# A trunk layer's second feed-forward half-step: one fp32 copy on another engine, and two pieces of work behind a later anchor

## The chip, the cores and the metric

The kernel runs on one core of a Trainium2 chip. A core has a matrix engine (TensorE, PE in the profile, with its weight loads shown as PEld), VectorE (DVE), ScalarE (ACT), GpSimd (POOL) and SyncE (SP), which here only issues DMAs. Each engine works through its own list of instructions in order and waits on semaphores for the others. The metric is the device time of one execution in microseconds (us); of several runs the median counts.

## The reference

One layer of a diffusion trunk on 512 latent and 128 context tokens, model width 1024: a half-step SwiGLU feed-forward, a token mixer (differential attention beside a chunkwise mLSTM), and a second half-step SwiGLU. Each stage is modulated by shifts, scales and gates that come from a conditioning vector. The change lies at the entry of the second half-step, which is

```python
hh = rmsnorm(x, g[2]) * (1 + m[7]) + m[6]
x = x + 0.5 * m[8] * swiglu(hh, p['ffn2_w1'][l], p['ffn2_w3'][l], p['ffn2_w2'][l])
...
def swiglu(h, w1, w3, w2):
    return (jax.nn.silu(h @ w1) * (h @ w3)) @ w2
```

with an inner width of 2816. All arrays are fp32.

## The kernel before

**Layout.** Activations lie transposed: feature d of the model in 8 tiles of 128 partitions, the 640 tokens along the free dimension, cut in two halves of 320 (`HALF`). The second half holds 192 latent and 128 context tokens, which have different shifts and scales; so `SEGS` (line 27) cuts every modulated operation of the second half in two, 192 and 128 long. The residual lies in four pair tiles (`x_pairs`, line 1764), each two feature tiles.

**Three matmuls for one.** TensorE works on rounded values (`F32R`). Each operand is split into a high part (a rounded copy, ScalarE) and a low part (value minus high part, VectorE), and `mm3` (line 133) or `into` (line 393) multiplies high by high, high by low and low by high. A value's low part needs the value itself in fp32 and its high part.

**The feed-forward.** The inner width is cut into 11 blocks of 256. Block 0 is done plainly: four sums (two column groups f, two weight matrices i) for each token half, each over 8 feature tiles k with three matmuls each (`plain`, line 313). The later blocks 1 to 10 use a Strassen-Winograd scheme with seven products in place of eight (`products`, line 406): A11, S1, S2, A12, S3, A22, S4. The operands on the activation side are four quarters (2 halves of the features by 2 halves of the tokens) and four sums of them, S1 to S4 (`operand_sums`, line 330); these sums are made in place in the fp32 residual pairs, so an fp32 copy of the modulated activations must stand there first. `terms` makes one sum on VectorE and its high part on ScalarE; `low` makes its low part on VectorE. S4 is kept in the tiles of the quarter (0, 1), the first features of the second token half, which block 0's plain products read.

On the weight side a **granule** is one 256 column block of w1 or w3 (`Granule`, line 232): `load` fetches 1 MB into one of two `raw` buffers, `parts` makes the split weights `wB` and `wC` and edits `raw` into the weight sums, and `sums` splits those into `ww`. `split_at` is the VectorE instruction that ends `sums` (line 268). Granule i+1's `parts` and `sums` are issued in the midst of granule i's products. In the stream of TensorE the last two products of a granule, A22 and then S4, come inside the next granule: A11, S1, A22 of the one before, S2, S4 of the one before, A12, S3. A product is 12 matmuls. Copies u2 and u3 of a PSUM bank (`copy_of`, line 401) are taken by ScalarE between products that go on accumulating in the same bank (Y); the sum for S1 with u3 is read by VectorE out of bank Z before S4 is added there.

Outputs of a block are gated (`SO`, SiLU of one times the other), split into `g` (`store_g`, line 372) and stored to `g_dram`, from which the second matrix's part, the "down" products, reads them much later. The residual was stored to `x2_dram` before it was overwritten, and is read back into `x_pairs` (line 1870) for the same later part.

**Entry of the second half-step.** `out_units(hf)` (line 1812) makes the mixer's output projection for one token half, adds it to the residual and collects the squares for the norm. `normed(hf)` (line 1825) turns them into the reciprocal root `rs`, multiplies the pairs by it in place (line 1834, VectorE), and then for each feature tile and segment has ScalarE write, with shift and scale, the rounded copy into `hm` (line 1838) and the fp32 copy in place (line 1839); VectorE subtracts the two for the low part of a pair (line 1841). `normed(1)` is issued after the first k of block 0's plain products for the first token half; the products for the second half follow.

**What sets the order.** TensorE's instructions keep the program's order (`keep_in_program_order`). For the other engines a scheduler orders the instructions by its own estimate of the times; `issue_after(x)` holds instructions of x's engine behind x. In `operand_sums` every VectorE instruction but the last two, the lows of S4, is chained to the one before it; the low of S2's second half is handed on as `behind`, which holds the second granule's `parts`.

Of the kernel before, what the change touches and what calls it, by code (L numbers as in the profile page):

```python
# [10 lines left out]
AF = mybir.ActivationFunctionType  # L11
ALU = mybir.AluOpType
# [19 lines left out]
def tile_trunk(ctx: ExitStack, tc: tile.TileContext, a: dict):  # L32
    nc = tc.nc
    act = nc.scalar.activation
# [9 lines left out]
    def ts(out, in0, s1, op0, s2=None, op1=None):  # L44
        if s2 is None:
            vec.tensor_scalar(out=out, in0=in0, scalar1=s1, scalar2=None, op0=op0)
        else:
            vec.tensor_scalar(out=out, in0=in0, scalar1=s1, scalar2=s2, op0=op0, op1=op1)
# [55 lines left out]
    scale = cp.tile([128, 3, KT, 2], F32, name="scale")  # L104
# [118 lines left out]
    A11, S1, S2, A12, S3, A22, S4, A21 = range(8)  # L223
# [71 lines left out]
    class HalfStep:  # L295
# [31 lines left out]
            act(s, p[0], AF.Silu)  # L327
            tt(vec, self.SO[:, self.Q[f, hf]], p[1], s, ALU.mult)

        def operand_sums(self, pair):  # L330

            SS = {i: self.fp.tile([128, 2, 4, HALF], F32R, tag=f"s{i}", name="S") for i in (S1, S2, S3)}
            SS[S4] = self.part[0, 1]
            self.ops = {A11: self.part[0, 0], A12: self.part[1, 0], A22: self.part[1, 1], **SS}
            a = [[[pair(2 * kh + r)[:, :, half(hf)] for hf in range(2)] for kh in range(2)] for r in range(2)]

            places = {
                S1: ((1, 1), (0, 1), (1, 1), ALU.add), S3: ((0, 1), (0, 0), (0, 1), ALU.subtract),
                S2: ((0, 0), (1, 1), (0, 0), ALU.subtract), S4: ((1, 0), (1, 0), (0, 0), ALU.subtract),
            }  # L340
            prev = None

            def next_of_vec(*args):
                nonlocal prev
                with ExitStack() as st:
                    if prev is not None:
                        st.enter_context(tc.issue_after(prev.ins))
                    prev = tt(vec, *args)

            def terms(i, r):  # L350
                to, x_, y_, op = places[i]
                v, x_, y_ = (a[r][kh][hf] for kh, hf in (to, x_, y_))
                next_of_vec(v, x_, y_, op)
                act(SS[i][:, 0, 2 * r : 2 * r + 2], v, AF.Copy)

            def low(i, r):
                kh, hf = places[i][0]
                ks = slice(2 * r, 2 * r + 2)
                next_of_vec(SS[i][:, 1, ks], a[r][kh][hf], SS[i][:, 0, ks].bitcast(F32), ALU.subtract)

            for f, i, r in (
                (terms, S1, 0), (terms, S1, 1), (terms, S3, 0), (low, S1, 0), (terms, S2, 0), (low, S1, 1), (terms, S3, 1),
                (terms, S2, 1), (low, S2, 0), (low, S2, 1), (low, S3, 0), (low, S3, 1), (terms, S4, 0), (terms, S4, 1),
            ):
                f(i, r)
                if (f, i) == (low, S2):
                    behind = prev.ins
            low(S4, 0)
            low(S4, 1)
            return behind  # L370

        def store_g(self, SO, b):
# [191 lines left out]
                for f in range(2):  # L564
                    unit(G[-1], j, f, 1)

        def run(self, x, gate, final, behind=None):


            def nothing(*args):  # L570
                pass

            n = self.n_plain
            down = [Whole(n, self.fetch_w2(0, n, j)) for j in range(4)]

            up = self.ops
            at = [[up[i] for i in (A11, S1, S2, A12)], [up[i] for i in (S3, S4, A22)], None]

            def fetch(q, i, eng=nc.sync):
                b0, b1 = ((0, n), *GROUPS)[q]  # L580
                eng.dma_start(out=at[q][i][:, :, : b1 - b0].bitcast(F32), in_=self.g_dram[i, :, :, b0:b1, :])

            work = self.up_work()
            work[-1][3] = lambda i: {A11: lambda: fetch(0, 0), S1: lambda: fetch(0, 1), S2: lambda: fetch(0, 2), A12: lambda: fetch(0, 3)}.get(i, nothing)()
            self.products(work, nothing, down[:2], behind=behind)
            at[1] += [self.fp.tile([128, 2, 4, HALF], F32R, tag=tag, name="op") for tag in ("gA", "SO")] + at[0][:2]
            x = x()

            def down_done(q, j):
                def done(f, hf, p, u):  # L590
                    d = 2 * j + f
                    if u is not None:
                        p = self.add(p, u)
                    add_residual(x, p, d, hf, gate)
                    if q == 2:
                        final(d, hf)

                def used(i):
                    if q == 1 and j == 3 and i in moves:
                        fetch(2, moves[i], nc.gpsimd)  # L600

                return done, used

            last = [
                [Granule(b1 - b0, self.fetch_w2(b0, b1, j)), lambda i, q=q: at[q][i], *down_done(q, j)]
                for q, (b0, b1) in zip((1, 2), GROUPS) for j in range(4)
            ]
            at[2] = at[0][2:] + at[1][:5]

            moves = {A11: S2, S1: A12, S2: S3, A12: A22, S3: S4}  # L610
            for j in range(4):
                ahead = down[j + 2] if j < 2 else last[j - 2][0]
                loaded = ahead.load()
                with tc.issue_after(loaded):
                    for i in ((A11, S1), (S2, A12), (S3,), ())[j]:
                        fetch(1, i)
                if j < 3:
                    down[j + 1].split()
                else:
                    last[0][0].parts(self.fp)  # L620
                    last[0][0].sums()
                for hf in range(2):
                    for f in range(2):
                        p = acc_tile(self.psum)
                        for kh in range(2):
                            op = at[0][PLAIN_Q[kh, hf]]
                            for b in range(n):
                                w = [down[j].w(i, n * kh + b, f) for i in range(2)]
                                mm3(p, *w, op[:, 0, b], op[:, 1, b], kh + b == 0, kh == 1 and b == n - 1)
                        add_residual(x, p, 2 * j + f, hf, gate)  # L630
                    if (j, hf) == (3, 0):
                        for i in (A22, S4):
                            fetch(1, i, nc.gpsimd)

            def load_last(load=last[3][0].load):
                with tc.issue_after(load()):
                    for i in (A11, S1):
                        fetch(2, i)

            last[3][0].load = load_last  # L640
            self.products(last, nothing, prepared=True)
# [51 lines left out]
    with ExitStack() as ph:  # L693
# [9 lines left out]
        hs = HalfStep(1, fp, ntmp, psum, a["w1a"], a["w3a"], a["w2a"], FB)  # L703
# [197 lines left out]
        x = Now()  # L901
# [445 lines left out]
    with tc.issue_after(box["normed"]):  # L1347
# [7 lines left out]
        for i in range(2):  # L1355
            vec.tensor_tensor_reduce(
                out=tab0[:, 3, i, :], in0=lamv[:, 2 * i, :], in1=lamv[:, 2 * i + 1, :], op0=ALU.mult, op1=ALU.add,
                scale=1.0, scalar=0.0, accum_out=ldot[:, i : i + 1],
# [403 lines left out]
    out = ExitStack()  # L1762
    zp = out.enter_context(tc.tile_pool(name="yy", bufs=1))
    x_pairs = pairs("k", "x")
    x = [x_pairs[d // 2][:, d % 2, :] for d in range(KT)]
# [59 lines left out]
    def normed(hf):  # L1825

        if hf == 0:
            natural_log_exp()
        rs = st[hf].rstd(psum)
        c0 = hf * HALF  # L1830
        shift = m_of(6)
        for g in range(4):
            xs = x_pairs[g][:, :, half(hf)]
            tt(vec, xs, xs, rs[:, None, :].to_broadcast([128, 2, HALF]), ALU.mult)
            for d in (2 * g, 2 * g + 1):
                for s0, s1, j in SEGS[hf]:
                    by = dict(scale=scale[:, 2, d, j : j + 1], bias=shift[:, d, j : j + 1])
                    act(hs.hh(d, hf)[0][:, s0 - c0 : s1 - c0], x[d][:, s0:s1], AF.Identity, **by)
                    act(x[d][:, s0:s1], x[d][:, s0:s1], AF.Identity, **by)
            p = hs.part[g // 2, hf][:, :, 2 * (g % 2) : 2 * (g % 2) + 2]  # L1840
            tt(vec, p[:, 1], xs, p[:, 0].bitcast(F32), ALU.subtract)

# [22 lines left out]
                hs.plain(ps[f, i], W[i], f, 1, k)  # L1865
    for f in range(2):
        hs.gate_plain(f, 1, (ps[f, 0], ps[f, 1]))
    summed = hs.operand_sums(lambda r: x_pairs[r])
    for g in range(4):
        nc.sync.dma_start(out=x_pairs[g], in_=x2_dram[:, 2 * g : 2 * g + 2, :])  # L1870
    hs.store_g(hs.SO, 0)
    hs.run(
        lambda: x, half_m[:, 1], lambda d, hf: nc.sync.dma_start(out=a["y"][:, d, half(hf)], in_=x[d][:, half(hf)]),
        behind=summed,
    )


# [126 lines left out]
```

## Time and profile before

| | us |
|---|---|
| median of 3 runs | 1868.25 |
| the three runs | 1867.74, 1868.25, 1875.11 |
| span of the profiled execution, first to last instruction | 1872.4 |
| busy of that: TensorE / VectorE / ScalarE | 1812.7 / 1300.2 / 849.6 |
| block 0's plain products of the second token half, start to first granule | 1459.45 to 1481.20 |

For the profiled execution only the span is given, as its own time. The mean clock granted to TensorE was 0.988 of full speed.

A row of the timeline has start, length, engine, line of the kernel, operation, output and inputs with their shapes, the count of merged instructions, and in brackets how long the engine was idle before it and what ended that. Rows of grouped instructions have after the count the busy time in us, the mean of one in ns, and the idle time before them. Nearly all VectorE operations have the line of a small helper: 39 for two-tensor operations, 42 for scalar_tensor_tensor, 46 and 48 for tensor_scalar; `hm` rows are told apart by their tiles.

### The profile page before, as it was taken

Reading aid. Unit: us, or ns where it says so; the run is one execution under the profiler, and the core shown is the slowest. Engines: PE = TensorE matmul, PEld = TensorE weight load, DVE = VectorE, ACT = ScalarE, POOL = GpSimd, SP = SyncE. Lnnn points to the kernel's source line nnn. Section 1 sums busy time; section 2 is a strip of 40 time slices with the busy share of each in tenths; the row PEclk is TensorE's granted clock in tenths of the full one; section 3 lists DMA queues with packets and bytes.
Section 4 is the critical chain, followed back from the end, with each engine's and each line's share of the span. In section 5 each row is a group of like instructions: output and inputs, shape, how many; then the busy total and the mean of one; then the engine's idle time right before and its main releaser. Section 6 shows DMA issues by size and latency. Waiting matters only on the chain.

```text
span 1872.4 us, 30753 instructions
## 1 busy us (share of the span) xinstructions
PE 1812.7 (97%) x12658; PEld 1774.4 (95%) x12658; DVE 1300.2 (69%) x2177; ACT 849.6 (45%) x1455; POOL 35.8 (2%) x57
## 2 busy tenths in 40 slices
PE   5899999999999999999999989999999999999999
PEld 4899999999998999999999979999999899999999
DVE  6888886576786675865755537875456778887585
ACT  5644444112554353453454436565235645554232
POOL 1000001110000000000000000000000000000000
PEclk8899999999999999999999999999999999999999
DMA  8344547964324322322222254566442344457972
GB/s 328 119 142 168 192 169 260 382 213 146 118 81 133 123 74 95 120 77 95 98 79 83 74 178 128 187 208 218 167 134 95 130 140 153 171 177 250 336 275 91
DMA packets 127293, 299.81 MB, mean 160 GB/s; under 512 B 9457, under 2 KB 90609, under 8 KB 114353
## 3 DMA queue, kind: packets, MB, share of 16 engines
q1 hardware_dynamic: 117890, 257.49, 40.0%
q0 software_dynamic: 9264, 40.37, 5.9%
q8 instruction: 99, 1.62, 0.4%
q14 instruction: 40, 0.33, 0.0%
HBM read 234.20 MB, written 63.63 MB: 159 GB/s over the span
## 4 chain that ended last, share of the span: by engine, by line
PE 86%; DVE 7%; DMA 4%; ACT 2%; issue 1%; SPq 0%; DVEq 0%; ACTq 0%
PE ps_f L52 41%; PE ps_p L52 22%; PE ps_t L52 12%; PE ps_o L52 2%; PE sc L52 2%; PE ps_n L52 2%; PE ps_u L52 1%; DMA ada<-csil_dram 1%; PE ps_wT L55 1%; DVE ww L39 1%; PE ps_qkT L55 1%; DMA P<-nm_dram 1%; DMA so<-o_dram 0%; DVE wL L39 0%; DMA raw_a<-in_w_ada_c 0%
## 5 line engine op out<-in xcount | busy, mean ns | idle before, releaser
L52 PE MATMUL ps_f<-S,ww 128*128 128x320 f32 x1992 | 322.9, 311 | 6.7 <-ACT ww L267 4.2
L52 PEld LDWEIGHTS ps_f<-S,ww 128*128 128x128 f32 x1992 | 301.1, 189 | 9.7 <-ACT ww L267 4.5
L52 PE MATMUL ps_p<-hH,wH 128*128 128x320 f32 x864 | 274.0, 317 | 3.1 <-ACT aT L1325 2.5
L52 PE MATMUL ps_p<-hH,wL 128*128 128x320 f32 x864 | 267.3, 309 | 0.0
L52 PE MATMUL ps_p<-hL,wH 128*128 128x320 f32 x864 | 267.2, 309 | 0.0
L52 PE MATMUL ps_f<-hm,ww 128*128 128x320 f32 x1248 | 198.2, 311 | 2.0 <-DVE ww L39 2.0
L52 PEld LDWEIGHTS ps_f<-hm,ww 128*128 128x128 f32 x1248 | 188.2, 190 | 2.3 <-DVE ww L39 2.2
L52 PE MATMUL ps_t<-wH,hH 128*128 128x256 f32 x640 | 185.7, 290 | 1.0 <-DVE x L42 1.0
L52 PE MATMUL ps_t<-wH,hL 128*128 128x256 f32 x640 | 181.8, 284 | 0.0
L52 PE MATMUL ps_t<-wL,hH 128*128 128x256 f32 x640 | 181.5, 284 | 0.0
L52 PEld LDWEIGHTS ps_p<-hH,wH 128*128 128x128 f32 x864 | 162.8, 188 | 4.4 <-ACT aT L1325 2.7
L39 DVE TENSOR_TENSOR ww<-raw,ww 128x2048 fp32r<-128x2048 f32 (+1 forms) x62 | 138.7, 2237 | 37.7 <-ACT ww L267 18.7
L52 PEld LDWEIGHTS ps_p<-hL,wH 128*128 128x128 f32 x864 | 162.8, 188 | 0.5
L52 PEld LDWEIGHTS ps_p<-hH,wL 128*128 128x128 f32 x864 | 162.5, 188 | 0.0
L52 PE MATMUL ps_f<-hm,wB 128*128 128x320 f32 x1008 | 161.5, 309 | 0.0
L52 PEld LDWEIGHTS ps_f<-hm,wB 128*128 128x128 f32 x1008 | 151.3, 188 | 0.0
L39 DVE TENSOR_TENSOR wL<-raw,wH 128x2048 fp32r<-128x2048 f32 x49 | 112.1, 2289 | 38.2 <-ACT wH L123 38.1
L123 ACT ACTIVATE wH<-raw 128x2048 fp32r<-128x2048 f32 x49 | 93.6, 1911 | 89.4 <-PE ps_p L52 85.5
L39 DVE TENSOR_TENSOR raw<-raw 128x1024 f32<-128x1024 f32 x144 | 124.6, 865 | 1.9
L52 PEld LDWEIGHTS ps_t<-wH,hH 128*128 128x128 f32 x640 | 123.1, 192 | 2.0 <-issue 1.2
L52 PEld LDWEIGHTS ps_t<-wH,hL 128*128 128x128 f32 x640 | 123.1, 192 | 0.5 <-DVE hL L42 0.5
L52 PEld LDWEIGHTS ps_t<-wL,hH 128*128 128x128 f32 x640 | 123.3, 193 | 0.2
(295 smaller groups left out, 3206.0 us busy)
## 6 DMA issues: line engine op xcount, KB each, us to landing
g_dram<-g SPq DMA_DIRECT2D x44, 640.0 KB, 5.1
raw_a<-in_w_ada_c SPq DMA_DIRECT2D x24, 512.0 KB, 4.0
raw<-in_w1b SPq DMA_DIRECT2D x11, 1024.0 KB, 4.9
raw<-in_w3b SPq DMA_DIRECT2D x11, 1024.0 KB, 4.8
raw<-in_w1a SPq DMA_DIRECT2D x10, 1024.0 KB, 4.8
raw<-in_w3a SPq DMA_DIRECT2D x10, 1024.0 KB, 6.4
ada<-in_w_ada_c POOLq DMA_DIRECT2D x18, 512.0 KB, 5.3
hm<-g_dram POOLq DMA_DIRECT2D x7, 1280.0 KB, 9.6
```

The costliest lines, as they stand in the source:

```text
L39: return eng.tensor_tensor(out=out, in0=in0, in1=in1, op=op)
L52: tc.keep_in_program_order(nc.tensor.matmul(*args, **kw))
L55: tc.keep_in_program_order(nc.tensor.transpose(*args, **kw))
L123: act(h, raw, AF.Copy)
```

## The change

Two edits. First, in `normed`, the fp32 copy of the modulated activations is made by ScalarE for the first token half, as before, and by VectorE (tensor_scalar, multiply and add with a scalar per partition) for the second: 16 instructions, two for each feature tile.

Second, `operand_sums` can hold back the two lows of S4 and hand them on as a function. `run` calls it in the first granule, at the point in `products` before S3, together with the reads of `x2_dram` and block 0's store (`store_g`), with VectorE's instructions of these held behind the second granule's `split_at`.

```diff
-        def operand_sums(self, pair):
+        def operand_sums(self, pair, hold=False):
...
-            low(S4, 0)
-            low(S4, 1)
+
+            def last():
+                low(S4, 0)
+                low(S4, 1)
+
+            if hold:
+                return behind, last
+            last()
             return behind
...
-        def run(self, x, gate, final, behind=None):
+        def run(self, x, gate, final, behind=None, after=None):
...
-            self.products(work, nothing, down[:2], behind=behind)
+
+            def between(i, at):
+                if (i, at) == (0, 1):
+                    with tc.issue_after(work[1][0].split_at):
+                        after()
+
+            self.products(work, between, down[:2], behind=behind)
...
-                    by = dict(scale=scale[:, 2, d, j : j + 1], bias=shift[:, d, j : j + 1])
-                    act(hs.hh(d, hf)[0][:, s0 - c0 : s1 - c0], x[d][:, s0:s1], AF.Identity, **by)
-                    act(x[d][:, s0:s1], x[d][:, s0:s1], AF.Identity, **by)
+                    xd, sc, sh = x[d][:, s0:s1], scale[:, 2, d, j : j + 1], shift[:, d, j : j + 1]
+                    act(hs.hh(d, hf)[0][:, s0 - c0 : s1 - c0], xd, AF.Identity, scale=sc, bias=sh)
+                    if hf == 0:
+                        act(xd, xd, AF.Identity, scale=sc, bias=sh)
+                    else:
+                        ts(xd, xd, sc, ALU.mult, sh, ALU.add)
...
-    summed = hs.operand_sums(lambda r: x_pairs[r])
-    for g in range(4):
-        nc.sync.dma_start(out=x_pairs[g], in_=x2_dram[:, 2 * g : 2 * g + 2, :])
-    hs.store_g(hs.SO, 0)
+    summed, last_lows = hs.operand_sums(lambda r: x_pairs[r], True)
+    SO = hs.SO
+
+    def after():
+        last_lows()
+        for g in range(4):
+            nc.sync.dma_start(out=x_pairs[g], in_=x2_dram[:, 2 * g : 2 * g + 2, :])
+        hs.store_g(SO, 0)
+
     hs.run(
         lambda: x, half_m[:, 1], lambda d, hf: nc.sync.dma_start(out=a["y"][:, d, half(hf)], in_=x[d][:, half(hf)]),
-        behind=summed,
+        summed, after,
     )
```

## The prediction

> **What bounds the kernel now.** I read the page's busy shares first, then the waits of TensorE, then its timeline where they lie.
>
> ```profile
> span 1872.4 us, 30753 instructions
> PE 1812.7 (97%) x12658; PEld 1774.4 (95%) x12658; DVE 1300.2 (69%) x2177; ACT 849.6 (45%) x1455; POOL 35.8 (2%) x57
> ```
>
> TensorE is busy for 97%, so an edit on VectorE and ScalarE is worth only what TensorE waits for them. The waits of TensorE from 1290 us to the end, and its busy time by stretches (length, PE busy and count, ... , granted clock):
>
> ```profile
> PE ps_f L52 <- DVE hm L39: 4.4, 2, 2.6
> ...
> 1463.00:1465.00 2.00, 0.81 (x6) 0.55 (x4) 0.49 (x1) 1.99 (x4) 0.00 (x0) 0.93 0.00 0
> 1465.00:1471.50 6.50, 5.05 (x17) 4.66 (x18) 5.89 (x9) 5.02 (x12) 0.00 (x0) 0.50 0.00 0
> ...
> 1481.20:1868.80 387.60, 387.60 (x2642) 387.11 (x2640) 290.19 (x386) 169.65 (x228) 4.93 (x7) 1.00 0.58 205
> ```
>
> Two waits, both for the low parts of the second token half (`hm`), and then 6.5 us at half clock. From 1481.2 us on TensorE is never idle, so what is saved ahead of that point reaches the end whole, unless new waits take it. The timeline of TensorE there:
>
> ```profile
> 1459.45 0.72 PE L52 MATMUL ps_f<-hm,wH 128*128 128x320 f32 x2
> ...
> 1460.59 0.31 PE L52 MATMUL ps_f<-hm,wH 128*128 128x320 f32 x1
> 1462.67 0.41 PE L52 MATMUL ps_f<-hm,wH 128*128 128x320 f32 x1 [1.77 <-DVE hm L39]
> ...
> 1463.50 0.31 PE L52 MATMUL ps_f<-hm,wH 128*128 128x320 f32 x1
> 1466.44 0.63 PE L52 MATMUL ps_f<-hm,wH 128*128 128x320 f32 x1 [2.63 <-DVE hm L39]
> ...
> 1471.51 0.47 PE L52 MATMUL ps_f<-hm,wH 128*128 128x320 f32 x2
> ...
> 1481.20 1.92 PE L52 MATMUL ps_f<-hm,wB 128*128 128x320 f32 x12
> 1482.96 3.68 PE L52 MATMUL ps_f<-S,ww 128*128 128x320 f32 x24
> ```
>
> At 1459.45 block 0's plain products of the second half begin: 4 chains x 8 k x 3 = 96 matmuls, ending at 1481.20 where the first granule's A11 begins. A product of 12 takes 1482.96 - 1481.20 = 1.76 us, so 96 should take 14.08 us. They take 21.75: **7.67 us are lost**, and that is all the change can win. Of it 4.40 is the two idle stretches; 2.58 is the 17 matmuls from 1466.44 to 1471.51, 5.07 us where 17/12 x 1.76 = 2.49 would do (about 0.4 of it a further wait for the last low part); the remaining 0.7 is lost around these stops.
>
> Why the low parts are late: ScalarE writes rounded and fp32 copies in turns, and each low part waits for both.
>
> ```profile
> 1452.14 1.76 ACT L1838 ACTIVATE hm<-x,mod,scale 128x192 fp32r<-128x192 f32 x4 [2.47 <-DVE x L39]
> 1453.80 0.53 ACT L1839 ACTIVATE x<-x,mod,scale 128x192 f32<-128x192 f32 x1
> ...
> 1462.60 1.28 ACT L327 ACT_TABLE_LOAD   x1
> 1463.89 0.44 ACT L327 ACTIVATE s<-ps_f 128x320 f32<-128x320 f32 x1
> ...
> 1451.28 3.03 DVE L39 TENSOR_TENSOR x<-x,ry 128x640 f32<-128x640 f32 x4
> ...
> 1465.56 0.83 DVE L39 TENSOR_TENSOR hm<-x,hm 128x640 fp32r<-128x640 f32 x1 [0.71 <-ACT x L1839]
> ...
> 1467.53 0.83 DVE L39 TENSOR_TENSOR hm<-x,hm 128x640 fp32r<-128x640 f32 x1
> ```
>
> **The change, part by part.** The two programs' instruction orders are equal on TensorE and GpSimd; VectorE, ScalarE and the DMA queue of SyncE differ only from `normed(1)` on, for some four granules.
>
> Durations (mean ns), all of 1444 to 1530 us but the first three, which come from the whole span:
>
> ```profile
> L46 DVE TENSOR_SCALAR fg<-lf 64x640 f32<-64x640 f32 x1 | 0.5, 486 | 0.0
> L42 DVE SCALAR_TENSOR_TENSOR x<-x,scale,ry 128x192 f32<-128x192 f32 x8 | 3.3, 411 | 0.0
> L42 DVE SCALAR_TENSOR_TENSOR x<-x,scale,ry 128x128 f32<-128x128 f32 x8 | 2.8, 345 | 0.0
> ...
> L39 DVE TENSOR_TENSOR S<-x,S 128x640 fp32r<-128x640 f32 x6 | 4.8, 821 | 0.1
> L39 DVE TENSOR_TENSOR ww<-raw,ww 128x2048 fp32r<-128x2048 f32 x5 | 11.4, 2290 | 5.4 <-ACT ww L267 5.4
> L267 ACT ACTIVATE ww<-raw 128x2048 fp32r<-128x2048 f32 x5 | 9.5, 1907 | 3.7 <-PE ps_f L52 3.0 <-DVE raw L39 0.8
> L39 DVE TENSOR_TENSOR raw<-raw 128x512 f32<-128x512 f32 x11 | 7.6, 689 | 0.2
> L39 DVE TENSOR_TENSOR wB<-raw,wB 128x1024 fp32r<-128x1024 f32 x6 | 7.3, 1221 | 1.0 <-ACT wB L252 1.0
> L39 DVE TENSOR_TENSOR raw<-raw 128x1024 f32<-128x1024 f32 x6 | 7.3, 1219 | 0.0
> L1839 ACT ACTIVATE x<-x,mod,scale 128x128 f32<-128x128 f32 x8 | 3.9, 483 | 0.0
> L39 DVE TENSOR_TENSOR SO<-ps_f,s 128x320 f32<-128x320 f32 x7 | 3.4, 487 | 2.5 <-ACT s L327 1.7 <-PE ps_f L52 0.7
> L39 DVE TENSOR_TENSOR g<-SO,g 128x1280 fp32r<-128x1280 f32 x2 | 3.0, 1488 | 0.0
> L381 ACT ACTIVATE g<-SO 128x1280 fp32r<-128x1280 f32 x2 | 2.5, 1270 | 2.1 <-DVE SO L39 2.1
> ```
>
> *Removed:* 16 fp32 copies from ScalarE (L1839). Its 16 rounded copies then run back to back; four start in 1453.80 - 1452.14 = 1.66 us, 0.415 each, so the sixteenth starts at 1452.14 + 15 x 0.415 = 1458.37 and ends at about 1458.85. The table load comes next, 1.28, and the two SiLUs of the first half end at 1460.6 and 1461.0.
>
> *Added:* 16 tensor_scalar copies on VectorE, after 1451.28 + 3.03 = 1454.31. This form, short and from SBUF, is not in the trace. One end: the same operation on 640 elements took 486 ns where a two-tensor operation took 821, a step per element about halved; with the rest of 821 (150 ns) as its fixed part that gives 0.25 us for 192 elements and 0.22 for 128, 3.7 us in all. Other end: the two scalar_tensor_tensor rows, 0.41 and 0.35, 6.0 us. I take the first, the same operation. In the new order a low part follows after the 7th, 11th and 16th copy, then two gate products (`SO`), then the last low part.
> - At 3.7 us VectorE keeps up with ScalarE: last copy 1459.1, third low part 1459.9, gate products behind the SiLUs 1461.1 and 1461.5, last low part 1462.35. TensorE wants that at matmul 19, 1459.45 + 19 x 0.147 = 1462.24. Wait: 0.1.
> - At 6.0 us the third low part ends at 1454.31 + 6.0 + 3 x 0.82 = 1462.8 (wanted 1461.36) and the last at 1464.6: waits of 2.4 together.
>
> I count 0.2. The plain products then end at 1459.45 + 14.08 + 0.2 = **1473.7**, 7.5 us earlier.
>
> *Moved:* S4's lows and block 0's store now wait on VectorE for the second granule's `ww`. Queued behind them there: the third granule's `wB`, then the sum that frees bank Z for S4's product. On ScalarE the rounding of block 0's output stands still *ahead* of that `ww`. On SyncE's queue the third granule's weights now go ahead of the reads of `x2_dram`. Every engine must now serve TensorE 7.5 us earlier.
> - First `ww`: nine 640-element operations from 1462.35, at 0.78 (3.03/4, rounded up), to 1469.4, and 2.29 to 1471.7. S1 starts at 1473.7 + 1.76 = 1475.5. No wait.
> - Second `ww`: ScalarE does it behind the SiLU of the first granule's A12, which starts at 1473.7 + 3 x 1.76 = 1479.0; a product's result is there 1.92 after its start, so 1480.95 with a handover. SiLU 0.44, or 0.35 until the next starts, then 1.91: 1483.2; VectorE's 2.29: 1485.55. VectorE's own work ahead (five 640s, `wB`, a `wC` priced as the 512 row, three edits of `raw`, two `SO`) is 4.1 + 1.22 + 0.69 + 2.6 + 0.97 = 9.6 from 1471.7, so `raw` is ready at 1481.3, no later than the SiLU. TensorE wants the low `ww` at S1's third matmul, 1473.7 + 6 x 1.76 + 0.3 = 1484.6. **Wait: 1.0.**
> - S4's lows: 1485.55 + 2 x 0.82 = 1487.2; then 1.49 for `g`, 1.22 for `wB`, 0.49 for the sum out of Z: 1490.4. S4 starts three products after that S1 starts, 1484.3 + 1.0 + 3 x 1.76 = 1490.6. No wait, by 0.2 us.
> - Third `ww`: after the sum out of Z come 0.69 + 1.22 + 0.69 (1493.0), S4's own sum (its result is there at 1492.6: 1493.5), the last edit of `raw` 0.69, then 1.91 and 2.29: 1498.4. TensorE wants it four products and 0.3 after S4's start, 1490.6 + 4 x 1.76 + 0.3 = 1497.9. **Wait: 0.5.** From the fourth on `raw` is ready before the engines reach it; I count nothing.
>
> Sum: 7.67 - 0.2 - 1.0 - 0.5 = **6.0 us**. The profiled execution's span would go from 1872.4 to 1866.4. It stands 4.15 above the median of the three runs (1868.25, from 1867.74 to 1875.11), and I take the same 6.0 off the median: **1862.3**.
>
> *The half clock.* The granted clock was still 0.93 between the two waits and fell to 0.50 in the second, when TensorE had been idle for most of 1460.7 to 1466.4 us. Single waits of 1.0 us or less should not bring it back, so its 2.2 us (2.58 less the 0.4 of waiting) count as gone.
>
> [...]
>
> **Rivals.**
> 1. *Given back behind VectorE and ScalarE.* The copies cost 6.0 us (2.4 of waits, not 0.2), and the second and third `ww` and the sum out of Z are each 1 us later: 2.4 + 2.0 + 1.5 + 1.0 = 6.9 of 7.67, so 1867.5. For it: margins of 0.1 and 0.2 us. Against: the nearest row is the same operation.
> 2. *The half clock is in the profiled execution alone.* The fall came only in the second wait; an execution in which it came later or not at all has 2.2 us less to win, and if the median run before is one, the gain is 3.8: 1864.5. For it: the profiled span is 4.15 above the median. Against: 4.4 us idle in less than 6 leave little room to miss. [...]
> 3. *Slower: the third granule's weights land late.* On ScalarE their rounding `wC` now stands ahead of S4's second high part, `g` and the copy u2 that frees bank Y for S3.
>
> ```profile
> 1482.30 0.33 SPq L74 DMA_DIRECT2D raw<-in_w1b  x1
> ...
> DMA to landing us min/median/max: 4.7/4.8/5.1
> ...
> L252 ACT ACTIVATE wC<-raw 128x512 fp32r<-128x512 f32 x6 | 3.8, 630 | 2.3 <-PE ps_f L52 2.0 <-PE ps_p L52 0.3
> L403 ACT ACTIVATE u<-ps_f 128x320 f32<-128x320 f32 x8 | 3.4, 429 | 1.5 <-PE ps_f L52 1.5
> ...
> L354 ACT ACTIVATE hm<-x 128x640 fp32r<-128x640 f32 x2 | 1.5, 741 | 2.2 <-PE ps_f L52 2.1
> ```
>
> Issued at 1471.7 they land at 1476.6; `wC` 0.63, the high part 0.74, `g` 1.27 and u2 0.43 end at 1479.7, and S3 starts at 1480.75: 1.0 to spare. Each microsecond more stops TensorE. Slower than before begins at a stop of 4 us with the half clock back (4.0 + 2.2 = 6.2, all of the 6.0), a landing 10 us after the issue. Sharing the engines with the two reads of `x2_dram` that follow, at a third of the rate, would be 14.7 us: a stop of 8.7, and 1868.25 - 6.0 + 8.7 + 2.2 = 1873.2. Against: no load here took over 5.1.
> 4. *The change does not do what it says.* The orders show that it does on VectorE; on ScalarE nothing is behind the sums, as told above. No chance of its own.
>
> **How the numbers follow.** Forecast (1860.5 to 1865) 0.65; rival 1 0.15; rival 2 0.10; rival 3 0.06; more than all of 7.67, by something unseen, 0.04. About 0.5% (9.3 us) is what a measurement of this kernel can tell from no change; the whole loss is 0.41%, so faster by more is 0.05, slower by more 0.04, within 0.91. The range: from 1859.5 (no new wait at all, 1860.6, and a median that moves by 1 us) to 1868.5 (rival 1 and the same).
>
> **What would show it.** ScalarE's 16 rounded copies without a gap, ending near 1459 (lead-in unchanged); tensor_scalar rows of about 0.25 and 0.22 us; A11 of the first granule near 1473.7; granted clock 1.00 throughout; one TensorE wait of about 1 us for `ww` near 1484.6. Wrong: copies at 0.35 to 0.41, a wait for `hm` over 1 us, a wait of ScalarE's `wC` for a DMA, or a clock of 0.50 again.

## The result, and the profile after

| | before | after |
|---|---|---|
| median of 20 runs, us | 1873.76 | 1867.72 |
| lowest and highest, us | 1867.74 to 1876.32 | 1862.24 to 1870.40 |
| span of the profiled execution, us | 1872.4 | 1866.7 |

After against before is **0.9972, 95% interval 0.9965 to 0.9979**: 5.2 us faster (3.9 to 6.6). The two medians alone differ by 6.0 us, inside this interval; where the text needs one number it takes 5.2. The profiled execution of after took 1868.63 us, 1.9 more than its span.

The page of after, its busy shares:

```profile
PE 1811.2 (97%) x12658; PEld 1773.0 (95%) x12658; DVE 1303.5 (70%) x2193; ACT 842.6 (45%) x1439; POOL 35.9 (2%) x57
```

VectorE has 16 instructions more (2177 to 2193), ScalarE 16 fewer (1455 to 1439): the copies have moved. TensorE's waits in after from 1420 us on (total, times, longest), and its busy time and granted clock (the third figure from the right) in block 0's plain products of the second half and in the two granules behind:

```profile
PE ps_f L52 <- DVE ww L39: 1.6, 1, 1.6
PE ps_f L52 <- DVE hm L39: 0.4, 1, 0.4
PE ps_f L52 <- ACT u L409: 0.2, 1, 0.2
```

```profile
1458.48:1473.26 14.78, 14.39 (x99) 14.08 (x97) 14.74 (x22) 8.40 (x12) 0.00 (x0) 1.00 0.10 27
1473.26:1508.74 35.48, 33.84 (x230) 33.43 (x229) 27.88 (x34) 18.94 (x26) 0.00 (x0) 1.00 0.53 190
```

The 4.4 us of waiting for `hm` are 0.4, the half clock is gone, and a wait of 1.64 us for the second `ww` is new. TensorE's timeline in after:

```profile
1458.48 0.46 PE L52 MATMUL ps_f<-hm,wH 128*128 128x320 f32 x2
...
1461.87 0.41 PE L52 MATMUL ps_f<-hm,wH 128*128 128x320 f32 x1 [0.39 <-DVE hm L39]
...
1473.26 1.92 PE L52 MATMUL ps_f<-hm,wB 128*128 128x320 f32 x12
...
1482.06 1.92 PE L52 MATMUL ps_f<-hm,wB 128*128 128x320 f32 x12
1483.82 0.46 PE L52 MATMUL ps_f<-S,ww 128*128 128x320 f32 x2
1485.91 1.73 PE L52 MATMUL ps_f<-S,ww 128*128 128x320 f32 x10 [1.64 <-DVE ww L39]
...
1496.28 1.92 PE L52 MATMUL ps_f<-hm,wB 128*128 128x320 f32 x12
...
1508.74 1.92 PE L52 MATMUL ps_f<-hm,wB 128*128 128x320 f32 x12
```

The rows at 1458.48, 1473.26, 1482.06, 1496.28 and 1508.74 start the plain products and the first to fourth granule's A11. I call the time from the first to the last **the section**. Without a loss it holds 96 matmuls (14.08 us), five products (8.80) and twice seven (12.32 each): 47.52 us. It took 55.44 in before (1459.45 to 1514.89) and 50.26 in after, 5.18 less, as much as the 5.2 of the timed runs. The rest of the two spans differs by the 0.97 us at which the section starts earlier and, behind it, by 0.45 the other way. The sections of the profiles below start anywhere from 1452.6 to 1461.6 us; so I compare sections, not spans.

Of the 0.97 us, 0.37 goes with the hold. In before, some 15 us ahead of the section, ScalarE's `wC` waits for TensorE; so the last squares for the norm (`nsq`) come late, and TensorE waits for them (ScalarE, then TensorE in before):

```profile
1443.98 0.63 ACT L252 ACTIVATE wC<-raw 128x512 fp32r<-128x512 f32 x1 [0.25 <-PE ps_p L52]
```

```profile
1446.49 0.81 PE L52 MATMUL ps_ss<-nsq,ones 128*128 128x320 f32 x2 [0.25 <-ACT nsq L181]
```

The copies alone (below) have TensorE's wait for `nsq` too (0.2 us in all); after and the other seven kernels with the hold have none, and in after `wC` runs at 1443.03 with no idle time ahead. Why the hold frees that buffer earlier was not followed. Its effect is that TensorE reaches the plain products sooner against the norm: ScalarE's first rounded copy of the second half starts 7.31 us ahead of them in before (1459.45 - 1452.14) and 6.94 us in after (1458.48 - 1451.54). I call this **the lead**.

Why the second `ww` is late, on ScalarE and on VectorE in after:

```profile
1475.90 0.62 ACT L252 ACTIVATE wC<-raw 128x512 fp32r<-128x512 f32 x1
...
1480.35 1.06 ACT L252 ACTIVATE wB<-raw 128x1024 fp32r<-128x1024 f32 x1 [1.18 <-PE ps_f L52]
1481.32 0.42 ACT L493 ACTIVATE s<-ps_f 128x320 f32<-128x320 f32 x1
1481.63 1.90 ACT L267 ACTIVATE ww<-raw 128x2048 fp32r<-128x2048 f32 x1
```

```profile
1476.89 2.67 DVE L39 TENSOR_TENSOR raw<-raw 128x1024 f32<-128x1024 f32 x3
1483.57 2.29 DVE L39 TENSOR_TENSOR ww<-raw,ww 128x2048 fp32r<-128x2048 f32 x1 [4.00 <-ACT ww L267]
```

`raw` was ready at 1479.56. But in ScalarE's list the third granule's `wB` comes first, and it waits until 1480.35 for TensorE to be done with that buffer; SiLU and `ww` queue behind it, and VectorE idles 4.0 us.

### The profile page after: what moved, and what is told of

Its sections match the earlier page's. It is cut to its first block, busy times and chain, and to the rows that moved or that the text cites. A ratio compares the mean times of both kernels' runs of the same rounds, so it can differ in the third digit from the quotient of the medians.

```text
span 1866.7 us, 30740 instructions
## 1 busy us (share of the span) xinstructions
PE 1811.2 (97%) x12658; PEld 1773.0 (95%) x12658; DVE 1303.5 (70%) x2193; ACT 842.6 (45%) x1439; POOL 35.9 (2%) x57
## 4 chain that ended last, share of the span: by engine, by line
PE 86%; DVE 7%; DMA 4%; ACT 1%; issue 1%; SPq 0%; DVEq 0%; ACTq 0%
PE ps_f L52 40%; PE ps_p L52 22%; PE ps_t L52 12%; PE sc L52 2%; PE ps_o L52 2%; PE ps_n L52 2%; DMA ada<-csil_dram 2%; PE ps_u L52 1%; DVE ww L39 1%; PE ps_wT L55 1%; PE ps_qkT L55 1%; DMA raw<-in_w2b 1%; DMA P<-nm_dram 1%; DMA raw_a<-in_w_ada_c 0%; DVE junk L688 0%
```

## The experiments

The theory: the change wins what the half-clocked, interrupted plain products lost, and the hold only keeps the second `ww` from taking it back. Rivals: the copies make the whole gain, and the hold is idle; or the hold makes it; and for the half clock, that any stop of this kind brings it. All sections in one table (us; "plain" is the plain products, ideal 14.08; waits are TensorE's):

| kernel | plain | section | waits in it | against before, 95% |
|---|---|---|---|---|
| before | 21.75 | 55.44 | `hm` 1.77, 2.63 | |
| after | 14.78 | 50.26 | `hm` 0.39, `ww` 1.64, u 0.2 | 0.9965 to 0.9979 |
| copies alone | 14.42 | 54.08 | `ww` 2.38, 1.77 | 0.9986 to 1.0007 |
| hold alone | 22.06 | 55.50 | `hm` 0.36, 1.78, 2.63 | 0.9993 to 1.0015 |
| slow copies | 15.89 | 50.04 | `hm` 1.39, `ww` 0.30 | 0.9959 to 0.9985 |
| `ww` first | 14.77 | 48.36 | `hm` 0.39 | 0.9951 to 0.9979 |
| low first | 14.13 | 49.62 | `ww` 1.64 | 0.9957 to 0.9981 |
| both first | 14.12 | 48.26 | `ww` 0.26 | 0.9959 to 0.9981 |
| wait of three | 17.12 | 52.19 | `hm` 2.71, `ww` 0.31, u 0.80 | one run |
| wait of six | 21.63 | 55.22 | `hm` 5.29 | one run |

**Copies alone.** The tail of the file is as in before, so that nothing is held.

```diff
-    summed, last_lows = hs.operand_sums(lambda r: x_pairs[r], True)
+    summed = hs.operand_sums(lambda r: x_pairs[r])
+    for g in range(4):
+        nc.sync.dma_start(out=x_pairs[g], in_=x2_dram[:, 2 * g : 2 * g + 2, :])
+    hs.store_g(hs.SO, 0)
...
-        summed, after,
+        behind=summed,
```

> The first edit alone: VectorE makes the 16 fp32 copies, S4's lows, the reads of x2_dram and block 0's store stay where they were. Theory: TensorE loses in block 0's second half only what it loses in the changed kernel (0.7 us against 7.67), so the first granule's A11 starts about 7 us earlier than before; but in this kernel's instruction order ScalarE's part of the second granule's ww stands behind the copy of bank Y for that granule, so the wait for ww near the second granule's S1 grows from 1.6 to about 4 us and may bring the half clock back (2 us more). Net 1 to 3.5 us faster than before, against 5 to 6 for both edits. Rival (the copies alone make the whole gain, the second edit does nothing): 5 to 6 us faster, a wait for ww of 1.6 us or less.

Measured: ratio 0.9996, 0.7 us faster (from 2.6 faster to 1.3 slower). TensorE's timeline of this kernel, and busy time and clock behind the second stop:

```profile
1475.83 1.92 PE L52 MATMUL ps_f<-hm,wB 128*128 128x320 f32 x12
...
1488.94 0.56 PE L52 MATMUL ps_f<-S,ww 128*128 128x320 f32 x2 [2.38 <-ACT ww L267]
1491.26 2.85 PE L52 MATMUL ps_f<-S,ww 128*128 128x320 f32 x10 [1.77 <-DVE ww L39]
```

```profile
1491.26:1496.10 4.84, 4.84 (x22) 4.84 (x23) 4.21 (x5) 0.00 (x0) 0.00 (x0) 0.65 0.59 217
```

The forecast of 1 to 3.5 us faster is missed, though the interval reaches into it; the longer wait and the half clock came as the theory had them. The plain products are even shorter than in after (14.42; the lead is before's 7.31), and the second `ww` takes most of it back: 4.15 us of waits and a clock of 0.65 behind them. VectorE and ScalarE of the same kernel show why:

```profile
1482.05 1.49 DVE L39 TENSOR_TENSOR g<-SO,g 128x1280 fp32r<-128x1280 f32 x1
...
1485.30 0.49 DVE L39 TENSOR_TENSOR s<-ps_f,u 128x320 f32<-128x320 f32 x1 [1.16 <-ACT u L409]
1485.71 0.68 DVE L39 TENSOR_TENSOR raw<-raw 128x512 f32<-128x512 f32 x1
```

```profile
1486.65 0.42 ACT L441 ACTIVATE ps_f<-ps_f 128x320 f32<-128x320 f32 x1 [0.35 <-PE ps_f L52]
1486.98 1.90 ACT L267 ACTIVATE ww<-raw 128x2048 fp32r<-128x2048 f32 x1
```

Two lows, `g` and a sum that waits for the copy u, and with it for TensorE, stand among the edits of `raw`, so the last edit ends at 1486.39, 10.56 us after the first granule's A11; in after it is 1479.56 - 1473.26 = 6.30. ScalarE's `ww` starts 11.15 after it against 8.37. That the copies make the whole gain falls.

**Hold alone.** Both halves' fp32 copies stay on ScalarE: `if hf == 0:` becomes `if hf < 2:`.

> The second edit alone: the copies stay on ScalarE, S4's lows and block 0's output stand behind the second granule's ww. Theory: the two waits for the low parts (4.4 us together) and the half clock after them are those of before, the first granule's A11 starts 21 to 22 us after block 0's second half; ww is not late, as it was not before (0.2). Within 1 us of before. Rival (unloading VectorE and SyncE ahead of the second granule is what gains): 3 to 6 us faster. [...]

Measured: ratio 1.0004. TensorE's timeline of this kernel:

```profile
1461.03 0.42 PE L52 MATMUL ps_f<-hm,wH 128*128 128x320 f32 x1 [1.78 <-DVE hm L39]
...
1464.80 0.64 PE L52 MATMUL ps_f<-hm,wH 128*128 128x320 f32 x1 [2.63 <-DVE hm L39]
```

The waits of before stand, the clock is half again for 6.83 us, and the section is 55.50: as the theory had it. So neither half of the change is worth more than its interval alone (by the ratios, 0.7 us faster and 0.7 slower), and together they are worth 5.2: one makes the gain, the other keeps it.

**Slow copies.** The 16 copies with the dearer operation.

```diff
-                        ts(xd, xd, sc, ALU.mult, sh, ALU.add)
+                        stt(xd, xd, sc, sh.to_broadcast([128, s1 - s0]), ALU.mult, ALU.add)
```

> Both edits, but the 16 copies on VectorE are made by the two-source form (scalar_tensor_tensor with the shift broadcast), the other end of the price in the prediction. Theory: 0.41 and 0.35 us each, about 2 us more in all after overlap; waits for the low parts of 1.5 to 2.5 us in place of 0.4, no half clock; the later engines follow, so the time is 1 to 2 us above the changed kernel, 3.5 to 4.5 below before. Rival (the price of the copies is hidden under ScalarE's rounded copies): within 0.5 us of the changed kernel, waits for the low parts of 0.4.

Measured: ratio 0.9972, as after. The interval (2.8 to 7.7 us faster) holds the forecast's 3.5 to 4.5 too; the section decides. It is 50.04, 0.22 under after's and not 1 to 2 above it: a miss. VectorE of this kernel, then the same place in after:

```profile
1450.43 2.19 DVE L42 SCALAR_TENSOR_TENSOR x<-x,scale,mod 128x192 f32<-128x192 f32 x7
1452.53 0.82 DVE L39 TENSOR_TENSOR hm<-x,hm 128x640 fp32r<-128x640 f32 x1
...
1458.16 0.83 DVE L39 TENSOR_TENSOR x<-x 128x640 f32<-128x640 f32 x1
1458.89 0.83 DVE L39 TENSOR_TENSOR hm<-x,hm 128x640 fp32r<-128x640 f32 x1
```

```profile
1453.63 2.01 DVE L48 TENSOR_SCALAR x<-x,scale,mod 128x192 f32<-128x192 f32 x7
1455.56 0.82 DVE L39 TENSOR_TENSOR hm<-x,hm 128x640 fp32r<-128x640 f32 x1
...
1460.99 0.82 DVE L39 TENSOR_TENSOR hm<-x,hm 128x640 fp32r<-128x640 f32 x1
```

From start to start seven copies take 2.10 us here and 1.93 in after, 0.30 and 0.28 each, and all sixteen 4.7 and 4.4. So the copies' price differs by a third of a microsecond; most of the longer `hm` wait (1.39 for 0.39) is the edit at 1458.16 (0.73), which the scheduler set ahead of the last low part. And in its order ScalarE does the second `ww` ahead of `wC`, `wB` and SiLU, so that wait is gone:

```profile
1477.55 1.91 ACT L267 ACTIVATE ww<-raw 128x2048 fp32r<-128x2048 f32 x1
1479.35 0.62 ACT L252 ACTIVATE wC<-raw 128x512 fp32r<-128x512 f32 x1
```

The two nearly cancel. So this run prices the operation only by its rows; in its time, the places that the scheduler chose in the engines' lists outweigh the operation.

**`ww` first.** ScalarE's second `ww` is put ahead of the third granule's `wC` and `wB` and of the SiLU.

```diff
-            act(t[0], flat, AF.Copy)
+            self.copy_at = act(t[0], flat, AF.Copy).ins
...
+                        if i == 1 and behind is not None:
+                            st.enter_context(tc.issue_after(gr.copy_at))
...
-                done(0, 0, X, None)
+                with ExitStack() as st:
+                    if i == 0 and behind is not None:
+                        st.enter_context(tc.issue_after(work[1][0].copy_at))
+                    done(0, 0, X, None)
```

> The changed kernel, and ScalarE's part of the second granule's ww is put ahead of the third granule's wB and wC and of the SiLU of the first granule's A12. In the profile of the changed kernel that ww began at 1481.63 behind wB, which waited for TensorE to free a buffer (1480.35); its input was ready at 1479.56. Theory: ww starts at about 1479.6, VectorE ends its part at about 1483.8, TensorE wants it at 1484.1: the wait of 1.64 us goes, the time is 1 to 1.7 us below the changed kernel (about 0.36% below before). Rival (VectorE, with S4's lows behind ww, sets the pace): a wait of the same length comes one or two products later, for S4's lows, bank Z or the third ww, and the time is that of the changed kernel.

Measured: ratio 0.9965. ScalarE and TensorE of this kernel:

```profile
1474.36 1.91 ACT L267 ACTIVATE ww<-raw 128x2048 fp32r<-128x2048 f32 x1 [0.42 <-DVE raw L39]
...
1476.49 1.05 ACT L252 ACTIVATE wB<-raw 128x1024 fp32r<-128x1024 f32 x1
```

```profile
1478.58 1.92 PE L52 MATMUL ps_f<-S,ww 128*128 128x320 f32 x12
```

`ww` now waits only for `raw`, S1 of the second granule runs through, and the section is 1.90 shorter than after's: the cause of the wait for the second `ww` is shown.

**Low first, and both.** In the first of these two kernels VectorE's gate products of block 0 stand behind the last low part; in the second, that and `ww` first.

```diff
-            tt(vec, self.SO[:, self.Q[f, hf]], p[1], s, ALU.mult)
+            with ExitStack() as st:
+                if behind is not None:
+                    st.enter_context(tc.issue_after(behind))
+                tt(vec, self.SO[:, self.Q[f, hf]], p[1], s, ALU.mult)
```

> The changed kernel, with block 0's gate products (SO) of the first half held behind the last low part of the second half. In the profile of the changed kernel those two gate products waited behind the table load and the SiLUs and pushed the last low part to 1460.99, for a TensorE wait of 0.39 us. Theory: the last low part follows the third at once, the wait for hm is gone, and the wait for ww stays near 1.6 us (TensorE, ScalarE and VectorE all move 0.4 us earlier): about 0.4 us below the changed kernel, which a timing of some 2 us cannot show, but its profile can: no wait for hm. Rival (the last low part is bound by ScalarE's sixteenth rounded copy): the wait for hm stays at 0.3 to 0.4.

> Both reorderings on top of the changed kernel: the last low part ahead of the gate products, and the second granule's ww ahead on ScalarE. Theory: no TensorE wait over 0.2 us between block 0's second half and the fourth granule; from the start of block 0's second half to the first granule's A11 14.1 us, and on to the second's, the third's and the fourth's 8.8, 12.3 and 12.3 us; the time is 1.5 to 2.1 us below the changed kernel, 0.36 to 0.40% below before. Rival (VectorE becomes the bound with nothing left between): a new wait of 0.5 us or more for S4's lows, bank Z or the third ww.

Measured: ratios 0.9969 and 0.9970. TensorE's stop at the second `ww`, first in low first, then in both first:

```profile
1486.46 1.73 PE L52 MATMUL ps_f<-S,ww 128*128 128x320 f32 x10 [1.64 <-DVE ww L39]
```

```profile
1486.99 1.73 PE L52 MATMUL ps_f<-S,ww 128*128 128x320 f32 x10 [0.26 <-DVE ww L39]
```

Without the `hm` wait the plain products take 14.13 and 14.12, so after's 0.70 over the ideal is this one wait of 0.39 and its restart. Both first has the shortest section, 2.0 under after's, as its theory had it, but for a wait of 0.26 at `ww` where it allowed 0.2. The timed runs can't tell `ww` first, low first and both first from after: the intervals overlap.

**Wait of three, wait of six.** The last pair's low part is written three times, or six times, so that TensorE has one stop in place of before's two.

```diff
-            tt(vec, p[:, 1], xs, p[:, 0].bitcast(F32), ALU.subtract)
+            for _ in range(3 if (g, hf) == (3, 1) else 1):
+                tt(vec, p[:, 1], xs, p[:, 0].bitcast(F32), ALU.subtract)
```

> The changed kernel with the last low part written three times over (the same values), so that TensorE stops once, for about 2.7 us, where before it stopped twice, 1.77 and 2.63 us. [...]

> The same with the last low part written six times over: one stop of about 5 us. [...]

TensorE's stop and the time behind it, three first, then six:

```profile
1461.81 0.41 PE L52 MATMUL ps_f<-hm,wH 128*128 128x320 f32 x1 [2.71 <-DVE hm L39]
```

```profile
1461.81:1473.20 11.39, 11.39 (x78) 11.39 (x78) 11.28 (x15) 7.63 (x10) 0.00 (x0) 1.00 0.11 18
```

```profile
1460.87 0.64 PE L52 MATMUL ps_f<-hm,wH 128*128 128x320 f32 x1 [5.29 <-DVE hm L39]
```

```profile
1460.87:1465.27 4.40, 4.40 (x16) 4.40 (x17) 4.40 (x6) 2.54 (x4) 0.00 (x0) 0.50 0.00 0
```

A stop of 2.71 us cost itself and 0.33 more (17.12 - 14.08 - 2.71), at full clock; I call the 0.33 restart. Half of it is how idle time is counted: the record of a matmul lasts 0.31 us, but in a full stream the next one starts 0.147 after it. One of 5.29 halved the clock: 16 matmuls in 4.40 us, where 16 x 0.147 = 2.35 would do, so 2.05 on top. Of the 7.67 us that before lost, then, 4.4 are waits and some 2.2 their echo in the clock, as the prediction had it. That any stop of over 2.5 us brings the half clock falls. Each of the two kernels was run once.

## Why the prediction was right or wrong

**Right: the mechanism and the size.** The rounded copies run in one row, and the table load follows at once (ScalarE in after):

```profile
1451.54 6.71 ACT L1850 ACTIVATE hm<-x,mod,scale 128x192 fp32r<-128x192 f32 x16 [2.47 <-DVE x L39]
1458.27 1.28 ACT L327 ACT_TABLE_LOAD   x1
```

The forecast had them start at 1452.14 and end at 1458.85, the same 6.71. It set the first granule's A11 at 1473.7 (it came at 1473.26, from a start 0.97 earlier), the clock at 1.00 throughout, and one wait of about a microsecond for the second `ww`. It said a gain of 6.0; the runs give 5.2 (3.9 to 6.6). That 1867.72 lies in its range is luck: the forecast's own 1860.5 to 1865 missed it, and it stands where the first rival (1867.5) would have it, though that rival did not happen.

**Wrong: what can be told from no change.** The step that failed is "About 0.5% (9.3 us) is what a measurement of this kernel can tell from no change", and with it 0.91 for "within". The single runs of each kernel spread over more than 8 us, but twenty of each side give an interval of 0.07% either way: 0.28% is clear of no change. The prediction gives no reason for its bound; the three runs that it had of before spread over 7.4 us, which may have suggested it. The runs showed that a gain of 5.2 us can be told from none. With 0.65 for a gain of about 6 us, faster was the likely outcome by the forecast's own reasons.

**The level.** 1868.25 was the median of three runs of before; that of twenty is 1873.76. The forecast took its 6.0 off a median that was 5.5 too low, so 1862.3 is 5.4 under 1867.72. Its remark that the profiled span stood 4.15 above the median was the sign: the span was ordinary, two of the three runs low.

**The terms.** The forecast left 0.2 + 1.0 + 0.5 = 1.7 us of the loss; after's section lost 50.26 - 47.52 = 2.74, and before's had 0.25 more than the 7.67.
- *Last low part:* 0.70, not 0.2. The low part ended 3.33 us after the plain products began (1461.81 - 1458.48), where the forecast had 2.90; 0.37 of this is the lead, which the forecast took as unchanged. The copies alone have before's lead: there the low part ended after 2.98 us and the plain products lost 0.34 (14.42 - 14.08), near the 0.2. The copies were priced at 0.25 and 0.22 us, 3.7 in all; their rows in after are

```profile
L48 DVE TENSOR_SCALAR x<-x,scale,mod 128x192 f32<-128x192 f32 x8 | 3.0, 373 | 0.0
...
L48 DVE TENSOR_SCALAR x<-x,scale,mod 128x128 f32<-128x128 f32 x8 | 2.7, 340 | 0.0
```

but one starts 0.28 us after the other, since each begins before the last has ended: 4.4 in all, not 3.7 and not the 6.0 of the other end. Of these 0.7 us little reached TensorE, since the forecast had the gate products wait for the SiLUs, and in after they follow the third low part with no idle time.
- *Second `ww`:* 1.90 (a wait of 1.64, the rest restart), not 1.0. The forecast had found the right instruction, and the SiLU ahead of it, whose input it set at 1480.95. It did not count the third granule's `wB`, which stood ahead of both, could not start before 1480.35 for its buffer, and took 1.06.
- *Third `ww`:* no wait, not 0.5; that granule loses 0.14 by a wait put down to u.
- *S4's lows, the sum out of Z, the loads:* no wait, as forecast.

**The rivals.** *Given back behind VectorE and ScalarE* did not happen in after, but the copies alone are such a kernel, by another place: 4.15 us of waits at the second `ww`. *The half clock is in the profiled execution alone* would have made 3.8 us, a ratio of 0.9980, just outside the interval; and both profiles that have the two waits, before's and hold alone's, have the half clock. *The third granule's weights land late* fell: `wC` ran at 1475.90 with no idle time ahead. *The change does not do what it says* falls by the two halves taken singly; but the forecast's note that ScalarE's work is not behind the sums is where the 1.64 us came from.

**Open.** What moves the level of both kernels by 8 us from run to run. Part of it may be the granted clock: both first's profile has a mean clock of 0.988 and its section starts at 1461.59, wait of six's has 0.992 and 1452.58; and of after's twenty runs the five fastest have a mean clock of 0.994, the five slowest of 0.991. Hold alone, with 0.992 and 1457.44, fits less well, and no run tests it. Whether `ww` first, low first or both first beat after by the 0.6 to 2.0 us that their sections show. Why the lead goes with the hold. Some profiles have a later wait of TensorE for a DMA (`hm` from `g_dram`) of 0.6 to 1.0 us, others, before and after among them, none; it wasn't followed. From what length of stop on the clock falls to half, and whether it falls in every execution, was not shown.

## What to carry to other kernels

When work leaves a busy engine, look for the next instruction on which the end depends, and read what stands ahead of it in each engine's own list: here the second half of the change was worth nothing alone and made nearly all the difference between 0.7 and 5.2 us. Price a chain of short instructions by their starts, not by the mean of one, and count a stop of TensorE at more than its length: stops of 0.39, 1.64 and 2.71 us cost 0.31, 0.26 and 0.33 more here. Judge what can be measured from the interval of many runs, not from the spread of three.

## What the runs showed of the hardware

The stretches of half clock that could be read lasted about 3.4, 6.8 or 10.2 us. By the granted clock in steps of half a microsecond or one, in before:

```profile
1464.50:1465.00 0.50, 0.00 (x0) 0.00 (x0) 0.35 (x1) 0.50 (x2) 0.00 (x0) 0.71 0.00 0
...
1471.50:1472.00 0.50, 0.50 (x5) 0.50 (x5) 0.50 (x1) 0.50 (x1) 0.00 (x0) 0.97 0.00 0
```

and in the copies alone:

```profile
1491.00:1492.00 1.00, 0.74 (x3) 0.74 (x4) 1.00 (x2) 0.00 (x0) 0.00 (x0) 0.76 0.00 0
...
1494.00:1495.00 1.00, 1.00 (x6) 1.00 (x5) 0.93 (x3) 0.00 (x0) 0.00 (x0) 0.54 1.09 459
```

A mean of 0.71 over half a microsecond, between one at 1.00 (1464.00 to 1464.50) and one at 0.50 (1465.00 to 1465.50), I read as full clock to 1464.71, and so on: in before the clock was half from 1464.71 to 1471.53, 6.82 us; in hold alone and in the wait of six it was 6.83 each; in the copies alone from 1491.52 to 1494.92, 3.40. The last is half of the others, and it began 0.26 us after the wait was over. Read in the same way, the stretches ahead of this one in before's profile begin at 24.28, 82.31, 358.79, 679.64, 853.72 and 1116.54 us and last 3.41, 6.83 or 10.24 us.

| kernel | TensorE's stops, us | work between, us | granted clock |
|---|---|---|---|
| before | 1.77, 2.63 | 1.14 | 0.50, from 0.90 into the second stop |
| hold alone | 0.36, 1.78, 2.63 | 1.14 each | 0.50, from 0.76 into the third stop |
| copies alone | 2.38, 1.77 | 0.56 | 0.50, from 0.26 after the second stop |
| wait of six | 5.29 | | 0.50, from 2.82 into the stop |
| wait of three | 2.71 | | 1.00 |
| after, at `ww` | 1.64 | | 1.00 |

So in these sections the clock fell with stops of 4.15 to 4.77 us in all close together and with one of 5.29, and not with one of 1.64 or 2.71. Before's two waits, with the half clock behind them, were seen in two profiles, its own and hold alone's.
